# Sums of weight blocks by accumulating transfers in a seven-product FFN on one Trainium2 core

## The chip, the cores and the metric

The kernel runs on one core of a Trainium2 chip. The core has a matrix engine (TensorE, PE in the profile; its weight loads are PEld), VectorE (DVE), ScalarE (ACT), GpSimd (POOL) and SyncE (SP), which here only issues transfers. Sixteen DMA engines carry out the transfers of all queues. The metric is device microseconds of one execution; lower is better.

## The reference

One decoder layer over 256 tokens of width 2048: a SwiGLU FFN with half residual, a token mixer, a second such FFN, and a final norm. All is float32.

```python
D_MODEL = 2048; SEQ = 256; D_FF = 5632
def swiglu_ffn(x, w_gate, w_up, w_down):
    return (jax.nn.silu(x @ w_gate) * (x @ w_up)) @ w_down

x = x + 0.5 * swiglu_ffn(rms_norm(x, ffn1_norm), ffn1_w_gate, ffn1_w_up, ffn1_w_down)
z = rms_norm(x, mix_norm) @ w_in          # 2048 -> 5120, then RG-LRU and short conv
...
x = x + y @ w_out
x = x + 0.5 * swiglu_ffn(rms_norm(x, ffn2_norm), ffn2_w_gate, ffn2_w_up, ffn2_w_down)
return rms_norm(x, final_norm)
```

The change touches the two FFNs alone, and in them the products with the three weight matrices.

## The kernel before

**Precision by splitting.** A float32 matrix is split into a high part (ScalarE casts it to fp32r, the tiles `hi_`) and the rest (VectorE subtracts, the tiles `lo_`). A product is then made of three matmuls: both parts of the activations with the high part of the weights, and the high part of the activations with the low part of the weights. Weights are loaded in tiles of 512 rows by 512 columns (128 partitions x 4 x 512, 1 MB; a "unit" is 512 rows) by `load`, which issues one transfer on SP's queue; `parts_of` casts in two halves on ScalarE and makes the low part in one VectorE instruction of 2048 columns. Three sets of split tiles take turns (`splits_of`). Raw tiles come from a pool of three (`raws`) and, for the two that are kept and changed in place, a pool of two (`kept`, called w11 and w12).

**Blocks of seven products.** The FFNs take two token tiles (128 tokens each) by two units by two column tiles of 512 columns as a 2 x 2 by 2 x 2 block product, and make it with seven products of one token tile by one unit by one column tile where eight are usual. This needs sums of activations (made once, by `seven_of`) and sums of weights (made for each block, by `seven`). The weights of a block are w11, w12 (first unit, columns 0 and 1) and w21, w22 (second unit). Beside the seven products the block takes the remaining one or two units in the usual way (`usual`, both token tiles at once, the tiles `_x`), into the same four PSUM banks a, c, e, d. The order on PE is: product 0, product 4, usual 0 (columns 1), product 5, usual 1 (columns 1), product 6, product 2, usual 0 (columns 0), product 3, usual 1 (columns 0), product 1. The two `usual` calls of the second unit are left out where a block has one other unit. A product is 12 matmuls of 512 columns, 8 with the high and 4 with the low part; a usual unit is 24.

**The sums of weights before.** Product 4 takes w12 − w11, in place in w11 and in two halves of 1024 columns; product 5 takes w22 − that, again in w11; product 6 takes w22 − w12, in place in w12; product 3 takes w21 − w11, in place in w11. All five instructions are VectorE's. In the profile they are the TENSOR_TENSOR groups that write `raw_g`, `raw_u`, `raw_d` or `raw_g_first` from two raw tiles. The results of products 5 and 6 are copied from bank a to SBUF by ScalarE (`snap`: u2 and u3) and added later by `done`.

**How many.** For each FFN, ten blocks are gate and up products (columns 512 to 5632 in pairs, two other units each) and three are of the down projection (`down`, called after the first, third and fifth pair of columns; the first has one other unit, the later ones two). The first 512 columns of gate and up and part of the down projection are made without sums. That is 26 blocks in the kernel, 2 of them with one other unit.

**Order and waits.** A planner turns the program into one instruction list for each engine; each engine then runs its list in order and waits on semaphores. Nearly all instructions go through one helper, so their line in the profile is L43; SP's loads are L165 (`load`) and L208 (`part`, the transposes). GpSimd issues ten small transfers at the start (L109) and four memsets in the mixer. `order=True`, in two gate blocks of each FFN, pins a few VectorE instructions to program order; `ready` hands the first block of FFN 1 its w11 already split.

Of the kernel before, what the change touches and what calls it, by code (L numbers as in the profile page):

```python
# [13 lines left out]
AF = mybir.ActivationFunctionType  # L14
ALU = mybir.AluOpType
AX = mybir.AxisListType

P = 128
# [6 lines left out]
CW = 512  # L25
NC_D = D // CW
UK = 4
# [22 lines left out]
def hybrid_block(ctx: ExitStack, tc: tile.TileContext, a: dict, out: bass.AP):  # L50
    nc = tc.nc
    Engine.pinned = False
    dve, act, pe = (Engine(tc, e) for e in (nc.vector, nc.scalar, nc.tensor))
# [29 lines left out]
    def bank(name):  # L83
        return psum.tile([P, 512], F32, tag="ps", name=name)

    def f32(ap):
        return ap.bitcast(F32)
# [71 lines left out]
    def load(src, name, pieces=((0, UK),), loaded=None, kept=False):  # L159
        if kept:  # L160
            raw = extra[1].tile([P, UK, CW], F32, tag="kept", name=f"raw_{name}", bufs=2)
        else:
            raw = raws.tile([P, UK, CW], F32, tag="raw", name=f"raw_{name}")
        for i, e in pieces:
            nc.sync.dma_start(raw[:, i:e, :], src[i * P : e * P].rearrange("(j p) c -> p j c", p=P))  # L165
            if loaded:
                loaded(i)
        return raw

    def splits_of(name):  # L170
        pool, bufs = splits, 2
        if extra:
            turn_of["split"] += 1
            if turn_of["split"] % 3 == 0:
                pool, bufs = extra[0], 1
        hi = pool.tile([P, UK, CW], F32R, tag="hi", name=f"hi_{name}", bufs=bufs)
        lo = pool.tile([P, UK, CW], F32R, tag="lo", name=f"lo_{name}", bufs=bufs)
        return hi, lo, [(hi[:, j, :], lo[:, j, :]) for j in range(UK)]

    def parts_of(raw, name, pieces=((0, 2), (2, UK)), split=None):  # L180
        hi, lo, blk = splits_of(name)
        for i, e in pieces:
            if split:
                split(i)
            act.copy(hi[:, i:e, :], raw[:, i:e, :])
            if split:
                dve.tensor_tensor(lo[:, i:e, :], raw[:, i:e, :], f32(hi[:, i:e, :]), op=ALU.subtract)
        if not split:
            dve.tensor_tensor(lo, raw, f32(hi), op=ALU.subtract)
        return blk  # L190
# [4 lines left out]
    def stationary(tile, t):  # L195

        return [(tile[:, j, t * P : (t + 1) * P], tile[:, j, S + t * P : S + (t + 1) * P]) for j in range(UK)]
# [33 lines left out]
    def multiply(targets, blk, apart=False, middle=None):  # L231


        more = dict(skip_group_check=True) if apart else {}
        for ps, st, begin, _ in targets:
            for j in range(UK):
                pe.matmul(ps, st[j][0], blk[j][0], start=begin and j == 0, stop=False, **more)
                pe.matmul(ps, st[j][1], blk[j][0], start=False, stop=False, **more)
        if middle:
            middle()  # L240
        for ps, st, _, end in targets:
            for j in range(UK):
                pe.matmul(ps, st[j][0], blk[j][1], start=False, stop=end and j == UK - 1, **more)
        if len(targets) == NT:
            onward()
# [114 lines left out]
    def seven_of(sf, x0, x1, v, spare, parts, steps=None):  # L360

        a11, a12, a21, a22 = v[0, 0], v[0, 1], v[1, 0], v[1, 1]
        parts = iter(parts)

        def split(i, q):
            hi, lo = next(parts)
            act.copy(hi, q)
            dve.tensor_tensor(lo, q, f32(hi), op=ALU.subtract)  # L370
            sf[i] = [(hi[:, j, :], lo[:, j, :]) for j in range(UK)]

        sf.update({0: stationary(x0, 0), 1: stationary(x1, 0), 3: stationary(x1, 1)})
        dve.tensor_tensor(spare, a21, a22, op=ALU.add)
        split(4, spare)

        def adds():
            dve.tensor_tensor(a21, a11, a21, op=ALU.subtract)
            dve.tensor_tensor(a11, spare, a11, op=ALU.subtract)

        def rest():
            if steps is None:
                adds()
            split(5, a11)
            split(6, a21)
            dve.tensor_tensor(a12, a12, a11, op=ALU.subtract)
            split(2, a12)

        if steps is not None:
            steps.extend((adds, rest))  # L390
        return rest
# [1 line left out]
    def quad(tile):  # L393
        return tile.rearrange("p (j c) -> p j c", j=UK)

    def seven(w, rows, cols, sf, xs, name, keep, done, between=None, ready=None, whole=True, order=False):


        a, c, e, d = (bank(f"ps_{name}_{n}") for n in "aced")

        def get(u, n, kept=False):
            src = w[u * UK * P : (u + 1) * UK * P, cols[n] : cols[n] + CW]
            return load(src, f"{name}_{u}{n}", kept=kept)

        (r0, r1), two = rows, len(xs) > 1
        w11, first = ready or (get(r0, 0, True), None)
        w12 = get(r0, 1, True)
        b2, w22 = get(xs[0][0], 1), get(r1, 1)
        b3 = get(xs[1][0], 1) if two else None
        a2, w21 = get(xs[0][0], 0), get(r1, 0)  # L410
        a3 = get(xs[1][0], 0) if two else None

        def snap(ps, n):
            s = keep(f"{n}_{name}")
            act.copy(s, ps)
            return s

        def product_of(i, raw, ps, begin=False, end=True, blk=None):
            multiply([(ps, sf[i], begin, end)], blk or parts_of(raw, f"{name}_p{i}"), True)

        def usual(i, raw, n, *targets):

            blk = parts_of(raw, f"{name}_x{i}{n}")
            multiply([(ps, stationary(xs[i][1], t), b, z) for ps, t, b, z in targets], blk, True)

        product_of(0, w11, a, True, blk=first)
        s1 = None if whole else snap(a, "s1")
        if whole:
            act.copy(d, a)
        hi, lo, blk = splits_of(f"{name}_p4")  # L430
        for i in (0, 2):
            o = slice(i, i + 2)
            dve.tensor_tensor(w11[:, o], w12[:, o], w11[:, o], op=ALU.subtract)
            act.copy(hi[:, o], w11[:, o])
        for i in (0, 2):
            o = slice(i, i + 2)
            ins = dve.tensor_tensor(lo[:, o], w11[:, o], f32(hi[:, o]), op=ALU.subtract)
            if order:
                tc.keep_in_program_order(ins)
        product_of(4, w11, c, True, blk=blk)  # L440
        s5 = snap(c, "s5")
        if between:
            between(0)
        usual(0, b2, 1, (e, 1, True, not two), (c, 0, False, False))
        if between:
            between(1)
        dve.tensor_tensor(w11, w22, w11, op=ALU.subtract)
        product_of(5, w11, a)
        u2 = snap(a, "u2")
        if between:  # L450
            between(2)
        if two:
            usual(1, b3, 1, (e, 1, False, True), (c, 0, False, False))
        ins = dve.tensor_tensor(w12, w22, w12, op=ALU.subtract)
        if order:
            tc.keep_in_program_order(ins)
        product_of(6, w12, a)
        u3 = snap(a, "u3")
        done(1, 1, e, [u3, s5])
        product_of(2, w22, c)  # L460
        done(0, 1, c, [u2])
        usual(0, a2, 0, (d, 0, not whole, False), (a, 1, False, False))
        dve.tensor_tensor(w11, w21, w11, op=ALU.subtract)
        product_of(3, w11, a, end=not two)
        if two:
            usual(1, a3, 0, (a, 1, False, True), (d, 0, False, False))
        done(1, 0, a, [])
        product_of(1, w21, d)
        done(0, 0, d, [] if whole else [s1])

    def ffn(tag, norm, after, opening=False):
        with (
# [252 lines left out]
            def down(last):  # L725
# [64 lines left out]
                if tag == 1 and m == 5:  # L790
                    prepare()
                seven(
                    wd, (m, n), (2 * CW, CW), sh, [(u, hidden[u]) for u in others], f"d{tag}_{m}", keep, add,
                    within,
# [79 lines left out]
    with tc.tile_pool(name="mixer", bufs=1) as mp, tc.tile_pool(name="mixw", bufs=2) as mw:  # L874
# [208 lines left out]
        def row_factor(u):  # L1083
# [4 lines left out]
        order = [  # L1088
            (lru_x, 0, 0), (lru_x, 0, 1), (sc_c, 3, 0), (lru_gate, 1, 0), (sc_x, 4, 0),
            (lru_gate, 1, 1), (sc_c, 3, 1), (sc_x, 4, 1), (sc_b, 2, 0), (sc_b, 2, 1),  # L1090
        ]
        for i, (use, piece, half) in enumerate(order):
            between = row_factor if i == 0 else None
            ps = inward(w_in, piece * (D // 2) + half * CW, nm.xT, f"in_{piece}_{half}", between)
# [10 lines left out]
        for c, g in [(0, 0), (1, 0), (0, 1), (1, 1), (2, 0), (2, 1), (3, 0), (3, 1)]:  # L1105
# [3 lines left out]
            ps = product(w_out, c, (2 * g, 2 * g + 1), yT.__getitem__, f"o{c}_{g}", turn if (c, g) == (0, 1) else None)  # L1109
# [104 lines left out]
```

## Time and profile before

| | |
|---|---|
| median of 3 runs | 1709.46 us (1708.25 to 1712.31) |
| profiled execution | 1709.04 us |
| its span | 1707.3 us |
| PE busy | 1690.1 us (99%), 7471 matmuls |
| DVE busy | 1456.5 us (85%) |
| ACT busy | 1206.9 us (71%) |
| POOL busy | 6.3 us |
| DMA, SP's queue | 360.75 MB, 66.3% of 16 engines |
| HBM read | 339.82 MB |

Busy time is the time in which an engine had an instruction running. An engine that is off the path that sets the end may be busy without costing anything; what counts is who waits for whom. In a timeline row the first number is the start and the second the length in us, over as many instructions as "x" says; the bracket gives the idle time of the engine before it and what ended it.

### The profile page before, as it was taken

The page shows a single profiled execution, that of the slowest core. Times are in us where ns is not written, and L with a number is a line of the kernel's source. Part 1 is how long each engine was busy: PE and PEld are TensorE (multiplying, and loading weights), DVE is VectorE, ACT ScalarE, POOL GpSimd, SP SyncE. Part 2 cuts the span into 40 slices and gives each one's busy share as a digit, 9 for nine tenths or more (in the row PEclk, how much of TensorE's full clock was granted, in tenths as well). Part 3 has the DMA queues.
Part 4 walks back from the last instruction along what each step waited for, and adds up shares of the span by engine and source line. Part 5 has one row for each costly group of instructions (what it writes and reads, how often), then busy time and mean ns, then how long its engine had stood idle before and what let it go on. Part 6 is the DMA issues. An engine that isn't in the chain of part 4 may idle for free. (4 is left out here: it accounts for less than half of the span.)

```text
span 1707.3 us, 19494 instructions
## 1 busy us (share of the span) xinstructions
PE 1690.1 (99%) x7471; PEld 1394.7 (82%) x7471; DVE 1456.5 (85%) x1217; ACT 1206.9 (71%) x1501; POOL 6.3 (0%) x20
## 2 busy tenths in 40 slices
PE   8999999999999999999999999999999999999998
PEld 7888888888888888888888888888888888888886
DVE  7998988889889889668696679989989888889796
ACT  7867667776567678877877777685567765677764
POOL 1000000000000000000000000000000000000000
PEclk9999999999999999999999999999999999999999
DMA  8666567585567684875657694585666656576853
GB/s 307 205 230 197 197 222 222 182 276 189 191 202 206 233 270 131 258 216 191 213 190 221 191 301 161 198 271 185 222 213 205 220 188 222 197 216 203 248 196 123
DMA packets 254173, 363.11 MB, mean 213 GB/s; under 512 B 85892, under 2 KB 88320, under 8 KB 253952
## 3 DMA queue, kind: packets, MB, share of 16 engines
q1 hardware_dynamic: 253616, 360.75, 66.3%
q8 instruction: 58, 0.95, 0.2%
q10 hardware_dynamic: 144, 1.05, 0.2%
q14 instruction: 35, 0.29, 0.0%
q0 software_dynamic: 320, 0.07, 0.0%
HBM read 339.82 MB, written 2.10 MB: 200 GB/s over the span
## 5 line engine op out<-in xcount | busy, mean ns | idle before, releaser
L43 ACT CAST hi_u_p<-raw_u 128x1024 fp32r<-128x1024 f32 x140 | 141.5, 1047 | 56.8 <-DVE raw_u L43 27.1
L43 ACT CAST hi_g_p<-raw_g 128x1024 fp32r<-128x1024 f32 x132 | 134.0, 1047 | 57.8 <-DVE raw_g L43 26.1
L43 DVE TENSOR_TENSOR lo_u_p<-raw_u,hi_u_p 128x2048 fp32r<-128x2048 f32 (+1 forms) x80 | 160.0, 2019 | 14.7 <-ACT hi_u_p L43 14.2
L43 DVE TENSOR_TENSOR lo_g_p<-raw_g,hi_g_p 128x2048 fp32r<-128x2048 f32 (+1 forms) x75 | 151.7, 2031 | 20.4 <-ACT hi_g_p L43 19.7
L43 PE MATMUL ps_d<-hi_d,h 128*128 128x512 f32 x704 | 167.0, 389 | 0.0
L43 PEld LDWEIGHTS ps_d<-hi_d,h 128*128 128x128 f32 x704 | 132.1, 188 | 27.4
L43 PE MATMUL ps_in<-hi_in,xT_nm 128*128 128x512 f32 x640 | 151.9, 390 | 0.0
L43 PEld LDWEIGHTS ps_in<-hi_in,xT_nm 128*128 128x128 f32 x640 | 119.5, 188 | 24.6
L43 DVE TENSOR_TENSOR lo_in<-raw_in,hi_in 128x2048 fp32r<-128x2048 f32 x40 | 91.3, 2286 | 47.6 <-ACT hi_in L43 47.2
L43 ACT CAST hi_d_p<-raw_d 128x1024 fp32r<-128x1024 f32 x84 | 86.4, 1048 | 64.0 <-DVE raw_d L43 22.6
L43 DVE TENSOR_TENSOR lo_d<-raw_d,hi_d 128x2048 fp32r<-128x2048 f32 x44 | 100.2, 2288 | 34.0 <-ACT hi_d L43 33.9
L43 ACT CAST hi_u_x<-raw_u 128x1024 fp32r<-128x1024 f32 x80 | 81.2, 1047 | 38.6 <-PE ps_u_c L43 24.6
L43 DVE TENSOR_TENSOR lo_d_p<-raw_d,hi_d_p 128x2048 fp32r<-128x2048 f32 (+1 forms) x48 | 96.5, 2020 | 9.3 <-ACT hi_d_p L43 8.8
L43 ACT CAST hi_d<-raw_d 128x1024 fp32r<-128x1024 f32 x88 | 88.9, 1046 | 19.6 <-PE ps_d_d L43 7.6
L43 ACT CAST hi_in<-raw_in 128x1024 fp32r<-128x1024 f32 x80 | 80.8, 1046 | 30.3 <-PE ps_in L43 24.8
L43 DVE TENSOR_TENSOR raw_u<-raw_u,raw_u 128x2048 f32<-128x2048 f32 (+1 forms) x50 | 92.3, 1862 | 11.6 <-DMA raw_u<-in_ffn_w_up_dram 10.9
L43 DVE TENSOR_TENSOR lo_g_x<-raw_g,hi_g_x 128x2048 fp32r<-128x2048 f32 x40 | 91.4, 2285 | 9.2 <-ACT hi_g_x L43 9.1
L43 ACT CAST hi_g_x<-raw_g 128x1024 fp32r<-128x1024 f32 x80 | 81.2, 1046 | 22.3 <-PE ps_g_c L43 9.2
L43 DVE TENSOR_TENSOR lo_u_x<-raw_u,hi_u_x 128x2048 fp32r<-128x2048 f32 x40 | 91.4, 2284 | 1.3 <-ACT hi_u_x L43 1.1
L43 DVE TENSOR_TENSOR raw_g<-raw_g,raw_g 128x2048 f32<-128x2048 f32 (+1 forms) x46 | 84.9, 1868 | 4.7 <-DMA raw_g<-in_ffn_w_gate_dram 4.5
L43 PE MATMUL ps_d<-lo_d,h 128*128 128x512 f32 x352 | 87.3, 389 | 0.0
L43 PE MATMUL ps_in<-lo_in,xT_nm 128*128 128x512 f32 x320 | 79.0, 389 | 0.0
(402 smaller groups left out, 3661.4 us busy)
## 6 DMA issues: line engine op xcount, KB each, us to landing
raw_d<-in_ffn_w_down_dram SPq DMA_DIRECT2D x88, 1024.0 KB, 5.8
raw_u<-in_ffn_w_up_dram SPq DMA_DIRECT2D x87, 1024.0 KB, 5.3
raw_g<-in_ffn_w_gate_dram SPq DMA_DIRECT2D x86, 1024.0 KB, 5.3
raw_in<-in_w_in_dram SPq DMA_DIRECT2D x40, 1024.0 KB, 5.1
raw_o<-in_w_out_dram SPq DMA_DIRECT2D x16, 1024.0 KB, 5.9
xres<-in_x_dram SPq DMA_DIRECT2D x4, 512.0 KB, 7.6
raw_u<-in_ffn_w_up_dram SPq DMA_DIRECT2D x2, 512.0 KB, 9.3
raw_g_first<-in_ffn_w_gate_dram SPq DMA_DIRECT2D x1, 1024.0 KB, 12.0
```

Of the source, the lines that this page charges most:

```text
L43: ins = getattr(self.engine, name)(*args, **kwargs)
```

## The change

Signs are turned so that every sum of weights is an addition: the activations' sums take the other sign (`seven_of`: two instructions with another operator), and the results of products 5 and 6 are copied with a factor −1 (`snap` with `sign`, a scaled Copy on ScalarE in place of a copy). The sums of products 4 and 5 stay on VectorE. Those of product 6 (w12 += w22) and product 3 (w11 += w21) become accumulating transfers: `gather` issues, on GpSimd's queue, a transfer of the second weight tile from HBM that is added to the tile in SBUF. w22 and w21 are still loaded by SP as before, for products 2 and 1 and for the sum of product 5. The gather into w12 stands in the program ahead of product 4, that into w11 behind the snapshot of product 5. `fourth` has the default True, and no call passes another value. The pin of product 6's sum goes with its instruction.

```diff
@@ -371,7 +371,7 @@
             sf[i] = [(hi[:, j, :], lo[:, j, :]) for j in range(UK)]

         sf.update({0: stationary(x0, 0), 1: stationary(x1, 0), 3: stationary(x1, 1)})
-        dve.tensor_tensor(spare, a21, a22, op=ALU.add)
+        dve.tensor_tensor(spare, a21, a22, op=ALU.subtract)
         split(4, spare)

         def adds():
@@ -383,7 +383,7 @@
                 adds()
             split(5, a11)
             split(6, a21)
-            dve.tensor_tensor(a12, a12, a11, op=ALU.subtract)
+            dve.tensor_tensor(a12, a12, a11, op=ALU.add)
             split(2, a12)

         if steps is not None:
@@ -393,14 +393,19 @@
     def quad(tile):
         return tile.rearrange("p (j c) -> p j c", j=UK)

-    def seven(w, rows, cols, sf, xs, name, keep, done, between=None, ready=None, whole=True, order=False):
+    def seven(w, rows, cols, sf, xs, name, keep, done, between=None, ready=None, whole=True, order=False, fourth=True):


         a, c, e, d = (bank(f"ps_{name}_{n}") for n in "aced")

+        def of(u, n):
+            return w[u * UK * P : (u + 1) * UK * P, cols[n] : cols[n] + CW]
+
         def get(u, n, kept=False):
-            src = w[u * UK * P : (u + 1) * UK * P, cols[n] : cols[n] + CW]
-            return load(src, f"{name}_{u}{n}", kept=kept)
+            return load(of(u, n), f"{name}_{u}{n}", kept=kept)
+
+        def gather(to, u, n):
+            nc.gpsimd.dma_start(to, of(u, n).rearrange("(j p) c -> p j c", p=P), accum_op=ALU.add)

         (r0, r1), two = rows, len(xs) > 1
         w11, first = ready or (get(r0, 0, True), None)
@@ -410,9 +415,9 @@
         a2, w21 = get(xs[0][0], 0), get(r1, 0)
         a3 = get(xs[1][0], 0) if two else None

-        def snap(ps, n):
+        def snap(ps, n, sign=1.0):
             s = keep(f"{n}_{name}")
-            act.copy(s, ps)
+            act.activation(s, ps, AF.Copy, scale=sign)
             return s

         def product_of(i, raw, ps, begin=False, end=True, blk=None):
@@ -430,13 +435,14 @@
         hi, lo, blk = splits_of(f"{name}_p4")
         for i in (0, 2):
             o = slice(i, i + 2)
-            dve.tensor_tensor(w11[:, o], w12[:, o], w11[:, o], op=ALU.subtract)
+            dve.tensor_tensor(w11[:, o], w11[:, o], w12[:, o], op=ALU.add)
             act.copy(hi[:, o], w11[:, o])
         for i in (0, 2):
             o = slice(i, i + 2)
             ins = dve.tensor_tensor(lo[:, o], w11[:, o], f32(hi[:, o]), op=ALU.subtract)
             if order:
                 tc.keep_in_program_order(ins)
+        gather(w12, r1, 1)
         product_of(4, w11, c, True, blk=blk)
         s5 = snap(c, "s5")
         if between:
@@ -444,23 +450,23 @@
         usual(0, b2, 1, (e, 1, True, not two), (c, 0, False, False))
         if between:
             between(1)
-        dve.tensor_tensor(w11, w22, w11, op=ALU.subtract)
+        dve.tensor_tensor(w11, w11, w22, op=ALU.add)
         product_of(5, w11, a)
-        u2 = snap(a, "u2")
+        u2 = snap(a, "u2", -1.0)
+        if fourth:
+            gather(w11, r1, 0)
         if between:
             between(2)
         if two:
             usual(1, b3, 1, (e, 1, False, True), (c, 0, False, False))
-        ins = dve.tensor_tensor(w12, w22, w12, op=ALU.subtract)
-        if order:
-            tc.keep_in_program_order(ins)
         product_of(6, w12, a)
-        u3 = snap(a, "u3")
+        u3 = snap(a, "u3", -1.0)
         done(1, 1, e, [u3, s5])
         product_of(2, w22, c)
         done(0, 1, c, [u2])
         usual(0, a2, 0, (d, 0, not whole, False), (a, 1, False, False))
-        dve.tensor_tensor(w11, w21, w11, op=ALU.subtract)
+        if not fourth:
+            dve.tensor_tensor(w11, w11, w21, op=ALU.add)
         product_of(3, w11, a, end=not two)
         if two:
             usual(1, a3, 0, (a, 1, False, True), (d, 0, False, False))
```

## Prediction

> **What bounds the kernel now.** I read the page first (busy time, clock, DMA queues), then the waits of PE, then the windows of single blocks, then the timeline inside them. The page:
>
> ```profile
> span 1707.3 us, 19494 instructions
> ...
> PE 1690.1 (99%) x7471; PEld 1394.7 (82%) x7471; DVE 1456.5 (85%) x1217; ACT 1206.9 (71%) x1501; POOL 6.3 (0%) x20
> ...
> PEclk9999999999999999999999999999999999999999
> ```
>
> PE is busy for 1690.1 of 1707.3 us at full granted clock. The diff leaves every matmul in place, so a gain can only come out of the remaining 17.2 us. The waits of PE (who it waited for: us in total, times, longest) and the last matmul of the timeline split them:
>
> ```profile
> PE pt_n L43 <- DMA xres<-in_x_dram: 3.1, 1, 3.1
> PE pv_first L43 <- DMA rows_first<-in_ffn_norm_dram: 2.6, 1, 2.6
> PE ps_g_a L43 <- DVE lo_g_p L43: 1.5, 4, 0.4
> PE ps_u_c L43 <- DVE lo_u_p L43: 0.6, 1, 0.6
> PE ps_o L43 <- ACT hi_o L43: 0.3, 1, 0.3
> PE ps_o L43 <- DVE lo_o L43: 0.3, 1, 0.3
> PE ps_d_c L43 <- ACT s_d L43: 0.2, 1, 0.2
> 1697.70 1.07 PE L43 MATMUL ps_d<-lo_d,h 128*128 128x512 f32 x4
> ```
>
> The first two, 5.7 us, are the start; from 1698.8 to 1707.3 run 8.5 us of final norm and stores; neither is touched. 2.9 us are left in the middle, and only 2.1 of them (the two waits for DVE's lo_g_p and lo_u_p) lie in the blocks that change. DVE's 85% is thus a share of work hidden beside PE. Two blocks with four other loads and one with two (window, busy time and instructions of PE, PEld, DVE, ACT, POOL, then clock, DMA share, GB/s), and the DMA queue over the second:
>
> ```profile
> 200.46:241.26 40.80, 40.80 (x181) 33.78 (x180) 37.27 (x22) 25.53 (x30) 0.00 (x0) 1.00 0.61 206
> 241.26:282.06 40.80, 40.80 (x181) 33.78 (x180) 35.80 (x24) 27.42 (x31) 0.00 (x0) 1.00 0.68 219
> 1166.30:1196.20 29.90, 29.90 (x133) 24.60 (x132) 29.23 (x22) 19.85 (x24) 0.00 (x0) 1.00 0.64 210
> q1 hardware_dynamic: 6336, 8.91, 67.4%
> ```
>
> PE is busy for the whole of each, while DVE has some 10% and the DMA engines a third to spare.
>
> **The change, part by part.** There are 26 blocks: 24 of the long kind, and two short ones (the first `down` of each FFN, which has one other unit). *DVE.* A block now makes five sums, two of 1024 columns and three of 2048; the last two of the three leave DVE:
>
> ```profile
> L43 DVE TENSOR_TENSOR raw_u<-raw_u,raw_u 128x2048 f32<-128x2048 f32 x30 | 68.7, 2289 | 8.6 <-DMA raw_u<-in_ffn_w_up_dram 8.3
> L43 DVE TENSOR_TENSOR raw_g<-raw_g,raw_g 128x2048 f32<-128x2048 f32 x28 | 63.7, 2286 | 4.7 <-DMA raw_g<-in_ffn_w_gate_dram 4.5 <-DVE raw_g L43 0.2
> L43 DVE TENSOR_TENSOR raw_d<-raw_d,raw_d 128x2048 f32<-128x2048 f32 x18 | 41.2, 2290 | 1.8 <-DMA raw_d<-in_ffn_w_down_dram 1.4
> L43 DVE TENSOR_TENSOR raw_g_first<-raw_g,raw_g_first 128x2048 f32<-128x2048 f32 x2 | 4.6, 2282 | 0.0
> L43 DVE TENSOR_TENSOR raw_u<-raw_u,raw_u 128x1024 f32<-128x1024 f32 x20 | 23.6, 1222 | 3.0 <-DMA raw_u<-in_ffn_w_up_dram 2.7
> ```
>
> 30+28+18+2 = 78 = 26 x 3 wide sums, of which 52 go: 52 x 2.288 = 119 us, DVE from 1456 to about 1337 us. What that is worth on the path is bounded by 2.1 us. I take all of it: −2.1. *Signs.* Sum and difference in `seven_of` and the three sums that stay are the same instruction with another operator: 0. *Snapshots.* u2 and u3 become a scaled Copy:
>
> ```profile
> L43 ACT COPY u_u<-ps_u_a 128x512 f32<-128x512 f32 x20 | 11.6, 578 | 0.0
> L43 ACT ACTIVATE z<-ps_g_a 128x512 f32<-128x512 f32 x10 | 6.0, 600 | 31.3 <-PE ps_g_a L43 31.3
> L43 ACT CAST hi_u_p<-raw_u 128x1024 fp32r<-128x1024 f32 x140 | 141.5, 1047 | 56.8 <-DVE raw_u L43 27.1 <-issue 15.4 <-PE ps_u_a L43 12.0
> ```
>
> 52 x (600 − 578) ns = 1.1 us, hidden by ACT's idle third (25.53 of 40.80 us): 0; without that cover 1.1 us.
>
> *The gathers.* 52 accumulating transfers of 1 MB are added on POOL's queue; the plain loads of the same tiles stay on SP's, and none is moved. POOL has nothing else to do within the FFNs (its busy time is 6.3 us). Each gather is a new wait: for product 6 it starts when the two half sums have read w12, for product 3 when the low part of product 5 has been made, and the ACT casts of that product wait for its landing. Behind them in ACT's order stand the casts of the next units, behind those DVE's low parts, behind those PE; and the slot of w11 or w12, so SP's next kept load, comes free later by as much. How late may it land? After it come two casts (2 x 1.047 us) and a low part of 2.29 us, 4.4 us together, and PE needs the low part 1.8 us after the product's first matmul. From the timeline, the tightest regular block and the short one:
>
> ```profile
> 279.89 2.35 DVE L43 TENSOR_TENSOR raw_g<-raw_g,raw_g 128x1024 f32<-128x1024 f32 x2
> 292.92 2.29 DVE L43 TENSOR_TENSOR lo_g_p<-raw_g,hi_g_p 128x2048 fp32r<-128x2048 f32 x1 [0.31 <-ACT hi_g_p L43]
> 301.74 1.98 PE L43 MATMUL ps_g_a<-hi_g_p,xs 128*128 128x512 f32 x8
> 303.56 1.07 PE L43 MATMUL ps_g_a<-lo_g_p,xs 128*128 128x512 f32 x4
> 312.62 1.98 PE L43 MATMUL ps_g_a<-hi_g_p,x 128*128 128x512 f32 x8
> ...
> 1174.13 2.29 DVE L43 TENSOR_TENSOR lo_d_p<-raw_d,hi_d_p 128x2048 fp32r<-128x2048 f32 x1 [0.25 <-ACT hi_d_p L43]
> 1190.89 1.98 PE L43 MATMUL ps_d_a<-hi_d_p,h 128*128 128x512 f32 x8
> ```
>
> Product 6 starts at 301.74, its tile is free at 282.24: room 301.74 + 1.8 − 4.4 − 282.24 = 16.9 us. Product 3: 312.62 + 1.8 − 4.4 − 295.21 = 14.8 us. In the short block product 3 has 1190.89 + 1.8 − 4.4 − 1176.42 = 11.9 us. So 14.8 us (and twice 11.9) is the price limit of a gather. No row of this kernel shows an accumulating transfer. The nearest are plain loads and POOL's small ones (KB each, median us to landing):
>
> ```profile
> raw_g<-in_ffn_w_gate_dram SPq DMA_DIRECT2D x86, 1024.0 KB, 5.3
> raw_g_first<-in_ffn_w_gate_dram SPq DMA_DIRECT2D x1, 1024.0 KB, 12.0
> rows_first<-in_ffn_norm_dram SPq DMA_DIRECT2D x1, 8.0 KB, 1.7
> rows_many<-in_lru_conv_b_dram POOLq DMA_DIRECT2D x1, 4.0 KB, 6.0
> rows_conv<-in_lru_conv_w_dram POOLq DMA_DIRECT2D x1, 16.0 KB, 5.3
> ```
>
> Low end: 5.3 us, as a plain load: all hidden, even in the short blocks. High end: POOL's slowest small transfer and the slowest 1 MB load, 6.0 + 12.0 = 18.0 us: 24 x (18.0 − 14.8) + 2 x (18.0 − 11.9) = 89 us. Between them I take 5.3 us for POOL's path, and for 1 MB what a load takes beyond a small one on SP, 5.3 − 1.7 = 3.6 us, twice, as the old sum must be read as well as the weights: 5.3 + 7.2 = 12.5 us. It is nearer to the rows than the crowded 12.0 us, which is of the start, where everything is loaded at once. That is within 14.8; the short blocks lose 2 x (12.5 − 11.9) = 1.2 us.
>
> The collectives page of the Trainium skill (Collectives: The Full Stack, The bandwidth ceiling) gives the same reason for the doubling: an add inside a transfer is slow for its two source reads, not for the adding. By its measured ratio of 1.93 the landing would be 5.3 + 6.9 = 12.2 us, an estimate, and the short blocks would lose 0.6 us. No run here shows it yet.
>
> *The DMA engines.* 8.91 MB take 67.4% of a block, so 1.05 MB take 7.9%. Two gathers add 16% as plain traffic, to 83%, and 32% if doubled, to 99%. This counts waiting inside packets as work, so it is a ceiling; the loads' bursts can be moved by some us, as three sets of split tiles let ACT run ahead of PE. I take 0 and keep the full engines as a rival.
>
> **The sum.** −2.1 + 0 + 0 + 1.2 + 0 = −0.9 on the profiled execution's 1709.04 us (span 1707.3 and 1.7 us around it); the median of the runs is 1709.46, 0.4 more. So 1708.1 to 1708.6; I say 1708.6: no change that a measurement of this kernel could tell (0.2%, 3.4 us).
>
> **The rivals.** *Late gather (the other side).* Place: the cast of product 3, behind it PE. It decides from a landing of 14.8 us on, and every us beyond costs 24 us and more: at 16 us 24 x 1.2 + 2 x 4.1 = 37 us, 1746; at 18.0 us 1798. For it: the landing has no row, and POOL must write the descriptors of 512 rows of 2 KB where its small transfers had 8 to 32 rows. Against it: 2.3 us remain at my value. *Full DMA engines.* At 99% loads land late and each casts late; if 3% of a block were lost, 24 x 40.8 x 0.03 = 29 us, 1738; at a threefold price, 115%, 15% of it, 147 us, 1856. For it: the waits of DVE and ACT for landing weights that exist already (8.3 us of raw_u above). Against: a third of the engines' time is idle now. *The gain.* DVE relieved by 10% lets the split run further ahead, and all 2.9 us go without a new wait: 1709.0 − 2.9 = 1706.1; with luck in the start or end below the 0.2%. *DVE holds up POOL.* A POOL issue takes half a microsecond:
>
> ```profile
> 6.32 0.52 POOL L109 DMA_DIRECT2D rows_conv<-in_lru_conv_w_dram  x1 [0.55 <-DMA rows_many<-in_mix_norm_dram]
> ```
>
> If it advanced only while DVE is idle (some 12% of a block), it would take 0.52 / 0.12 = 4.3 us, the landing would be 12.5 + 3.8 = 16.3 us, and 24 x 1.5 + 2 x 4.4 = 45 us are lost: 1754. Against it: (2289 − 1222) ns for 1024 more columns is 1.04 ns a column, DVE's plain pace in these sums and low parts. SBUF — State Buffer in the Trainium skill (Who interferes with whom) has this lock: descriptors from GpSimd starve while DVE runs in a two-port mode, but tensor_tensor has no such mode; by that the rival falls, and no run here shows it.
>
> That the sums do not leave DVE at all can't be: the diff has no call with `fourth` off.
>
> **How the numbers follow.** Hidden 0.48; late gather 0.22; full engines 0.20; DVE's hold 0.05; gain 0.05. The last is faster, the three before it slower: faster 0.05, same 0.48, slower 0.47. The likeliest, hidden, gives 1708.6, its own range 1706.1 to 1712. The range goes up to 1765, which takes in all of DVE's hold and four fifths of the late gather and two thirds of the full engines (out: 0.04 and 0.07), and down to 1705.5 (out: 0.03).
>
> **What would show it.** Right: PE's waits in the blocks still a few us, DVE near 1337 us, 52 POOL transfers landing in 9 to 14 us, the DMA share of a long block 0.80 to 0.95. Wrong: PE waiting for hi_ or lo_ parts of products 3 and 6 with ACT waiting on a POOL transfer (late gather); waits spread over all products with ACT waiting on SP's loads (full engines); POOL issues of several us beside busy DVE (the hold).

## The result and the profile after

The changed kernel takes 1720.14 us (median of 5 runs, 1718.53 to 1725.6) against 1709.46: ratio 1.007 (1.0057 to 1.0084), 0.7% slower where no change was forecast. The page of its profiled execution (1720.14 us), the lines that answer to those of before:

```profile
span 1718.4 us, 19630 instructions
...
PE 1691.8 (98%) x7471; PEld 1394.0 (81%) x7471; DVE 1353.3 (79%) x1165; ACT 1204.9 (70%) x1501; POOL 73.8 (4%) x72
...
q1 hardware_dynamic: 253616, 360.75, 64.5%
q0 software_dynamic: 27776, 54.60, 19.0%
```

PE has the same work at a granted clock of 0.998 where it was 0.999 and stands idle 26.6 us instead of 17.2; its busy time is 1.7 us longer. VectorE lost 52 instructions and 103 us. What is new is queue q0, GpSimd's: 54.6 MB take 19.0% of the 16 engines' span. The waits of PE in the changed kernel (us in total, times, longest):

```profile
PE ps_u_c L43 <- ACT s_u L43: 6.3, 7, 2.4
PE pt_n L43 <- DMA xres<-in_x_dram: 3.5, 1, 3.5
PE pv_first L43 <- POOL ident masks.py:199: 2.5, 1, 2.5
PE ps_g_a L43 <- DVE lo_g_p L43: 2.0, 4, 0.7
PE ps_in L43 <- ACT hi_in L43: 1.5, 1, 1.5
PE ps_g_c L43 <- ACT s_g L43: 0.8, 1, 0.8
```

The start (pt_n, pv_first) is about as before, 6.0 us for 5.7; the middle grew from 2.9 to 12.0 us (1.4 of it in five smaller rows), and its largest entry is new: PE wants to write bank c again (`ps_u_c`) and ScalarE has not yet copied it out (`s_u`, the snapshot s5 of product 4). No row is a wait for the parts of product 3 or 6 (the waits for lo_g_p are product 5's, as before). Two neighbouring long blocks, gate and up, and the queues over the second (windows; columns as before):

```profile
204.06:244.86 40.80, 40.80 (x182) 33.79 (x180) 31.25 (x20) 24.13 (x29) 1.56 (x2) 1.00 0.87 257
244.86:287.03 42.17, 41.09 (x181) 33.71 (x180) 33.08 (x22) 27.96 (x32) 2.59 (x2) 1.00 0.94 262
q1 hardware_dynamic: 6339, 8.92, 64.0%
q0 software_dynamic: 1056, 2.10, 29.7%
```

The first block still takes 40.80 us, the second loses 1.37 us at a DMA share of 0.94. The transfers (issue to landing) and ScalarE's waits for them:

```profile
raw_d<-in_ffn_w_down_dram SPq DMA_DIRECT2D x88, 1024.0 KB, 6.3
raw_u<-in_ffn_w_up_dram SPq DMA_DIRECT2D x87, 1024.0 KB, 7.0
raw_g<-in_ffn_w_gate_dram SPq DMA_DIRECT2D x86, 1024.0 KB, 7.2
raw_u<-in_ffn_w_up_dram POOLq DMA_DIRECT2D x20, 1024.0 KB, 9.1
raw_g<-in_ffn_w_gate_dram POOLq DMA_DIRECT2D x19, 1024.0 KB, 9.3
ACT hi_g_x L43 <- DMA raw_g<-in_ffn_w_gate_dram: 20.7, 10, 4.1
ACT hi_u_x L43 <- DMA raw_u<-in_ffn_w_up_dram: 15.5, 7, 3.1
ACT hi_g_p L43 <- DMA raw_g<-in_ffn_w_gate_dram: 12.9, 6, 2.6
ACT hi_d_p L43 <- DMA raw_d<-in_ffn_w_down_dram: 3.9, 2, 2.5
```

The `_x` rows are SP's plain loads, of which those of raw_u and raw_g land 1.7 to 1.9 us later than before (5.3 us). The `_p` rows, with one more of 2.9 us for `raw_g_first`, are gathers: 19.7 us in nine waits, seven for product 3 in gate blocks, one for product 6 in the first short down block (1.4 us) and one for product 3 in the second (2.6 us).

### The profile page after: what moved, and what is told of

Its sections match the earlier page's. It is cut to its first block, busy times and chain, and to the rows that moved or that the text cites. A ratio compares the mean times of both kernels' runs of the same rounds, so it can differ in the third digit from the quotient of the medians.

```text
span 1718.4 us, 19630 instructions
## 1 busy us (share of the span) xinstructions
PE 1691.8 (98%) x7471; PEld 1394.0 (81%) x7471; DVE 1353.3 (79%) x1165; ACT 1204.9 (70%) x1501; POOL 73.8 (4%) x72
## 3 DMA queue, kind: packets, MB, share of 16 engines
q0 software_dynamic: 27776, 54.60, 19.0%
## 5 line engine op out<-in xcount | busy, mean ns | idle before, releaser
L43 PEld LDWEIGHTS ps_d<-lo_d,h 128*128 128x128 f32 x352 | 66.1, 188 | 13.7
L43 PEld LDWEIGHTS ps_in<-lo_in,xT_nm 128*128 128x128 f32 x320 | 60.1, 188 | 12.5
```

What stands on the lines that cost most here:

```text
L43: ins = getattr(self.engine, name)(*args, **kwargs)
```

## One stretch, followed from the gather to PE

The first gate block and the up block behind it show how the two reach PE. The rows of the changed kernel: POOL's issue of product 3's gather, rows of ScalarE and VectorE (timeline), the landing of the SP load issued at 76.86 us, and PE in the up block:

```profile
70.10 1.30 POOL L408 DMA_DIRECT2D raw_g_first<-in_ffn_w_gate_dram  x1 [10.42 <-DVE lo_g_p L43]
81.16 1.05 ACT L43 CAST hi_g_p<-raw_g_first 128x1024 fp32r<-128x1024 f32 x1 [2.86 <-DMA raw_g_first<-in_ffn_w_gate_dram]
87.14 2.00 ACT L43 CAST hi_g_x<-raw_g 128x1024 fp32r<-128x1024 f32 x2 [2.31 <-DMA raw_g<-in_ffn_w_gate_dram]
89.17 2.29 DVE L43 TENSOR_TENSOR lo_g_x<-raw_g,hi_g_x 128x2048 fp32r<-128x2048 f32 x1 [2.21 <-ACT hi_g_x L43]
93.97 0.60 ACT L43 ACTIVATE z<-ps_g_a 128x512 f32<-128x512 f32 x1 [0.52 <-PE ps_g_a L43]
103.75 1.99 ACT L43 CAST hi_u_p<-raw_u 128x1024 fp32r<-128x1024 f32 x2 [1.13 <-DVE raw_u L43]
106.60 0.59 ACT L43 ACTIVATE s_u<-ps_u_c 128x512 f32<-128x512 f32 x1
raw_g<-in_ffn_w_gate_dram SPq DMA_DIRECT2D x1, 1024.0 KB, 10.2
107.24 2.11 PE L43 MATMUL ps_u_c<-hi_u_x,x 128*128 128x512 f32 x8 [2.43 <-ACT s_u L43]
```

The gather lands 11.0 us after its issue and ScalarE stands 2.86 us; then a plain load, issued 6.8 us behind the gather, lands after 10.2 us and it stands another 2.31 us. ScalarE itself has made this up by `z` at 93.97, where it waits for PE. VectorE has not: from its low part of the late load at 89.17 to its sum for product 5 at 101.39 it is never idle for more than 0.13 us, so it hands the delay on. The casts of product 5 wait for that sum, the copy `s_u` stands behind them in ScalarE's list, and PE loses 2.43 us at bank c. All seven of PE's waits for `s_u` come behind such a wait for a plain load in the gate block ahead (1.6 to 4.1 us). The same rows of the kernel of e7, whose lists of instructions are in the same order and which waits for small transfers in place of the gather, 9.6 us from first issue to cast against 11.1:

```profile
69.99 1.29 POOL L410 DMA_DIRECT2D raw_g_first<-in_ffn_w_gate_dram  x1 [6.70 <-DVE lo_g_p L43]
79.64 1.05 ACT L43 CAST hi_g_p<-raw_g_first 128x1024 fp32r<-128x1024 f32 x1 [1.83 <-DMA raw_g_first<-in_ffn_w_gate_dram]
83.21 1.98 ACT L43 CAST hi_g_x<-raw_g 128x1024 fp32r<-128x1024 f32 x2
85.35 2.28 DVE L43 TENSOR_TENSOR lo_g_x<-raw_g,hi_g_x 128x2048 fp32r<-128x2048 f32 x1
93.58 0.60 ACT L43 ACTIVATE z<-ps_g_a 128x512 f32<-128x512 f32 x1 [3.39 <-PE ps_g_a L43]
100.41 2.00 ACT L43 CAST hi_u_p<-raw_u 128x1024 fp32r<-128x1024 f32 x2
103.25 0.60 ACT L43 ACTIVATE s_u<-ps_u_c 128x512 f32<-128x512 f32 x1
raw_g<-in_ffn_w_gate_dram SPq DMA_DIRECT2D x1, 1024.0 KB, 6.1
104.26 1.98 PE L43 MATMUL ps_u_c<-hi_u_x,x 128*128 128x512 f32 x8
```

Here the plain load lands after 6.1 us, ScalarE does not wait for it, and PE does not wait for `s_u`. Of the 3.8 us by which VectorE's low part is later in the changed kernel, 1.5 are there at the cast of product 3 already (81.16 against 79.64); the rest comes from the plain load.

## The experiments

Each ratio is to the kernel before, run beside it on the same chip (its medians there: 1708.94 for e1 to e4, 1708.66 for e5 to e8, 1709.15 for e9 to e12, 1708.63 us for e13 to e15).

**e1: the snapshot of bank c ahead of product 5's casts.**

```diff
-        s5 = snap(c, "s5")
+        s5 = keep(f"s5_{name}")
+        taken = act.activation(s5, c, AF.Copy, scale=1.0)
...
-        product_of(5, w11, a)
+        with tc.issue_after(taken.ins):
+            product_of(5, w11, a)
```

> The changed kernel with ScalarE's two casts of product 5 held behind the snapshot s5 of product 4 in ScalarE's order; nothing else is edited. Order theory: the 8.7 us that PE waits at the first use of bank c after product 4 come from the order alone, because the planner now puts these casts ahead of s5 in all ten up blocks; with s5 first they go, and the time falls to 1710 to 1713 us. Supply theory: the 54.6 MB of added traffic make every load late (5.3 to 7.0 us for raw_u), and s5 only happens to be where the lateness shows; the wait moves to the casts and low parts of product 5, and the time stays at 1717 to 1721 us.

1731.49 us, 1.0135 (1.012 to 1.0151). The order theory falls: with the snapshot early it is slower still. Product 5's casts come later, so w11 is free later, and in the up blocks product 3's gather is issued 8.2 us behind the first matmul of product 4 where it was 6.4 (medians, from the trace); ScalarE's waits for gathers grow from 19.7 to 58 us and those for SP's loads of the usual units (the `_x` rows) from 38 to 90 us. `s_u` looks like the place where the lateness came out, not its source; e1 alone does not show that, since it moves the gather too, but e7 does, with the list unchanged.

**e2: signs and scaled copies alone** (no gathers; both sums additions on VectorE).

```diff
-        gather(w12, r1, 1)
...
+        dve.tensor_tensor(w12, w12, w22, op=ALU.add)
         product_of(6, w12, a)
```

(and `fourth=False`, which puts the sum of product 3 back on VectorE.)

> The changed kernel with both gathers taken out and both sums made by VectorE again, as additions; the turned signs and the scaled copies stay. Both theories: 1708 to 1711 us, as before, since neither the order on ScalarE nor the traffic differs from the kernel before. If the scaled copies cost something on the path, 1711 us or more.

1709.22 us, 1.0004 (0.9995 to 1.0013): turned signs and scaled copies cost nothing that shows (at most 0.13%).

**e3: neither gathers nor sums for products 6 and 3.**

> The changed kernel without the gathers and without any sum for products 6 and 3, which take the tiles as they stand (the output is another one): VectorE is relieved as in the changed kernel, the traffic is that of before, and the planner again puts the casts of product 5 ahead of s5 in all ten up blocks. Order theory: PE still waits for s5, 6 to 9 us in all, 1715 to 1719 us. Supply theory: no late loads, no wait, 1706 to 1709 us. If it takes both, an order that is harmless as long as ScalarE is on time: 1707 to 1711 us.

1706.73 us, 0.9988 (0.9979 to 0.9997). This is what VectorE's relief is worth, 2.2 us, and about all that a version which moves these sums elsewhere has to gain.

**e4: only product 6's gather; e5: only product 3's** (the other sum on VectorE).

> The changed kernel with the gather of product 6 alone; the sum of product 3 is VectorE's. The order on ScalarE has the casts ahead of s5 in all ten up blocks, the added traffic is half. Order theory: 1716 to 1720 us, as the changed kernel. Supply theory: half of the loss, 1713 to 1716 us. Both needed: 1711 to 1716 us.

> The gather of product 3 alone; product 6's sum is an addition on VectorE again. Half the traffic, as in the kernel with product 6's gather alone (1710.3 us), but it is the gather whose landing ScalarE waited for: in the changed kernel the nine casts that waited for a gather (19.7 us of ScalarE's time in all) are nearly all of product 3. Wait theory (the loss is the landing of product 3's gather, late in ScalarE's order): most of the 11 us stays, 1716 to 1719 us. Traffic theory (the loss is the DMA engines' load by both gathers, and grows faster than the load): as product 6's gather alone, 1709 to 1711 us, with SP's loads of raw_g and raw_u landing in 5.3 to 5.8 us.

e4: 1710.33 us, 1.0009 (1.0 to 1.0017), although ScalarE waits 43 us for SP's plain loads there, more than the 38 of the changed kernel: the sum of such waits is no measure of the loss. e5: 1733.53 us, 1.014 (1.0125 to 1.0155), far beyond what either theory gave, and more than both gathers together. The two load the engines alike (q0 9.5% and 9.4%). In e5 ScalarE's list is another one, and it waits 57 us for gathers, in the up blocks too (`hi_u_p` 37.7 us, 10 times), where the changed kernel does not wait at all; there the gather is issued 10.0 us behind the first matmul of product 4 and not 6.4. So neither traffic nor the changed kernel's 19.7 us of waits is the whole account: the order that the planner makes decides when a gather starts and how much of its landing ScalarE sees.

**e6: gathers that overwrite instead of adding.**

```diff
-..., accum_op=ALU.add)
+...)
```

> Both gathers without the accumulation: each transfer overwrites its tile, so that the sums for products 6 and 3 are left out and the output is not the reference's. Every engine's instructions are those of the changed kernel, in the same order, with the same waits. If the DMA engines charge an accumulating transfer about double (19.0% of the span for 54.6 MB, against 64.5% for 360.75 MB), the gather queue's share falls to about 9.7%, and a transfer lands about 1 to 2 us earlier, in 7 to 8 us. Traffic theory: most of the loss goes, 1708 to 1712 us. Wait theory: a landing that is 1 to 2 us shorter takes away 9 to 18 us of the nine waits' 19.7 us, so that it too gives 1709 to 1713 us; what this run settles is the share of the loss that the accumulation itself causes. If it stays above 1716 us, neither the doubling nor the landing matters, but the count of transfers.

1712.48 us (1707.04 to 1716.62), 1.0016 (1.0006 to 1.0026). Same lists, same 1 MB transfers:

```profile
q0 software_dynamic: 14464, 54.60, 9.7%
raw_u<-in_ffn_w_up_dram POOLq DMA_DIRECT2D x20, 1024.0 KB, 5.6
```

Adding takes twice the packets and twice the engines' time (19.0% against 9.7%) and 3.5 us of landing. Without it no cast waits for a gather, SP's loads still land in 5.7 to 6.4 us and ScalarE still waits 27 us for them; 3.8 of the 10.7 us of loss are left, though its own runs lie 10 us apart.

**e7: the wait without the traffic**, two small accumulating transfers in a row for each gather.

```diff
+            src = of(u, n).rearrange("(j p) c -> p j c", p=P)
+            for _ in range(2):
+                nc.gpsimd.dma_start(to[:, :, :16], src[:, :, :16], accum_op=ALU.add)
```

> Wait without traffic: in place of each gather two small accumulating transfers one behind the other into 16 of the 512 columns of each row group (32 KB each, the second waits for the first, since they write the same place), so that the sums for products 6 and 3 are left out for the other columns and the output is not the reference's. The products' casts still wait for the landing of the second; from the small GpSimd transfers (5 to 6 us from issue to landing) two in a row should take 9 to 12 us, about what a whole gather took (9.1 us). Wait theory: the loss stays, 1716 to 1722 us. Traffic theory: SP's loads land in 5.3 us again and the time is that of the kernel with no gathers and no sums, 1706.5 to 1708.5 us.

1709.15 us, 1.0003 (0.9994 to 1.0011). ScalarE waits for gathers as in the changed kernel (19.6 against 19.7 us), and from first issue to last landing those of product 3 in the gate blocks take 10.5 us (median, from the issues and landings in the trace) against 10.3. In the up blocks and for product 6 the small pair is quicker than a gather (medians 7.5 against 10.2 us, and 6.4 to 6.9 against 8.6 to 8.7), but there ScalarE waits for gathers only once in the changed kernel, 1.4 us. SP's loads of raw_u and raw_g land in 5.3 and 5.4 us, ScalarE's waits for those of the usual units are gone, and so are 11.0 us. This is the cleanest comparison of the study: same lists, about the same waits for the gathers, without the bytes.

**e8: product 3 one unit later.**

```diff
-        product_of(3, w11, a, end=not two)
         if two:
-            usual(1, a3, 0, (a, 1, False, True), (d, 0, False, False))
+            usual(1, a3, 0, (a, 1, False, False), (d, 0, False, False))
+        product_of(3, w11, a)
```

> Traffic without product 3's wait: both gathers whole, but product 3 stands one unit (about 10 us of TensorE) later, behind the second other unit of the column, so that its cast has 10 us more before it needs the gather. Wait theory: 1708 to 1711 us. Traffic theory: 1716 to 1720 us. Side effect to be seen in the trace: w11's kept slot comes free some 10 us later, so that the next block's first load may be late; if the time is above 1722 us it is that, with ScalarE or VectorE waiting for SP's load ahead of product 0, and the run tells nothing on the two theories.

1771.35 us, 1.0363 (1.0349 to 1.0376). It is above 1722 us, the case set apart: by the edit w11's slot comes free one unit later, and VectorE, which does not wait for SP's loads in the changed kernel, does so here (`raw_u` 15.1 us; 10.9 in the kernel before). It tells nothing on the two theories.

**e9: three small transfers in a row.** The edit is e7's with `range(3)`.

> Wait without traffic, now as long as a whole gather: three small accumulating transfers in a row (32 KB each, one waits for the other) in place of each gather; the sums for products 6 and 3 are left out for the other columns, so that the output is not the reference's. Order of every engine as in the changed kernel. With two in a row (3.1 us median each) ScalarE waited 19.6 us for them, as long as for the whole gathers (19.7 us), and the time was 1709.15 us. Three take some 9.5 us, or up to 13 us where the first is delayed. Traffic theory: 1709 to 1712 us. Wait theory: 1716 us and more.

1836.61 us, 1.0745 (1.0727 to 1.0762): against the traffic theory, and the largest loss of all, while SP's loads of raw_u and raw_g land in 5.3 and 5.4 us. The first gate block (POOL's first issue, ScalarE's cast), and then the waits of PE:

```profile
73.10 1.29 POOL L410 DMA_DIRECT2D raw_g_first<-in_ffn_w_gate_dram  x1 [2.71 <-issue]
89.69 1.04 ACT L43 CAST hi_g_p<-raw_g_first 128x1024 fp32r<-128x1024 f32 x1 [8.30 <-DMA raw_g_first<-in_ffn_w_gate_dram]
PE ps_g_a L43 <- ACT u_g L43: 38.8, 9, 7.0
PE ps_u_a L43 <- ACT u_u L43: 31.6, 10, 5.0
```

With 16.6 us from first issue to cast (medians to the last landing 15.7 and 16.8 us in gate and up blocks) instead of 10 or 11 the wait becomes the bound. And PE does not wait for product 3's parts: it waits for `u_g` and `u_u`, the snapshot u3 of bank a, which stands behind the waiting cast in ScalarE's list. Not all of the loss is waiting: of the 126 us between the profiled executions of e7 and e9, 36 are PE's own busy time (1689.6 to 1725.4 us), at a granted clock of 0.979 against 0.998.

**e10: half gathers** (256 of 512 columns: `to[:, :, : CW // 2]`).

> Half the accumulating traffic, in the same order: both gathers, each for 256 of the 512 columns of a row group (512 KB), the other columns' sums left out, so that the output is not the reference's. Traffic theory: between the two small transfers (1709.15 us) and the whole gathers (1720.1 us), 1712 to 1716 us, with ScalarE's waits for SP's loads of raw_g and raw_u between 0 and 36 us. Wait theory: as the waits for the gathers go; a landing of about 7 us leaves the time at 1707 to 1710 us.

1708.54 us, 1.0 (0.9991 to 1.0008): 5.6 to 6.6 us for SP's loads, 6.0 us for a gather, no waits for gathers. Halving the transfers takes away the whole loss, not half of it; the traffic theory's 1712 to 1716 was too high.

**e11 and e12: the orders of e5 and e1 with two small transfers for each gather.**

> The kernel with product 3's gather alone (1733.5 us), its order of all engines kept, but two small transfers in a row (32 KB each) in place of the gather: no traffic, still a wait; product 3's sum is left out for the other columns, so that the output is not the reference's. If that kernel's order alone costs what it lost: 1725 us and more. If the order is only vulnerable, and the loads that collide with the gathers (SP's landing 6.2 to 6.5 us against 5.3) turn it into stalls: 1708 to 1712 us.

> The changed kernel with the snapshot of bank c put ahead of product 5's casts (1731.5 us), order kept, and two small transfers in a row (32 KB each) in place of each gather; the sums for products 6 and 3 are left out for the other columns, so that the output is not the reference's. The order alone at fault: 1722 us and more. Order only vulnerable to late loads and late gathers: 1707 to 1712 us.

e11: 1720.7 us, 1.0069 (1.0056 to 1.0083). e12: 1721.77 us, 1.0075 (1.0062 to 1.0089). Neither expectation was met: 12.8 and 9.7 us go with the traffic, and some 12 us stay. What stays comes with waits for the small transfers, 40 us of ScalarE's time in e11 and 73 in e12, at 9.5 to 11.5 us from first issue to last landing (medians of product 3's). No run has these lists without any gather, so it is not shown how much of the 12 us is the wait and how much the order by itself.

**e13: product 5's parts asked for earlier, gathers whole; e14: the same with two small transfers.**

```diff
+        dve.tensor_tensor(w11, w11, w22, op=ALU.add)
+        five = parts_of(w11, f"{name}_p5")
         usual(0, b2, 1, (e, 1, True, not two), (c, 0, False, False))
...
-        dve.tensor_tensor(w11, w11, w22, op=ALU.add)
-        product_of(5, w11, a)
+        product_of(5, w11, a, blk=five)
```

> The changed kernel with the sum, casts and low part of product 5 asked for ahead of the first other unit instead of behind it, so that w11 is free and the gather for product 3 starts about 3 us earlier in the gate blocks. Both gathers whole. If ScalarE's waits for the gathers (19.7 us in the changed kernel) are needed for the loss, it goes with them: 1708 to 1712 us. If the late loads alone carry it (ScalarE's waits for SP's loads of the FFNs' weights 38 us in the changed kernel): 1716 to 1722 us, with the waits for the gathers near 0.

> The same early order of product 5, with two small transfers in a row (32 KB each) in place of each gather; the sums for products 6 and 3 are left out for the other columns, so that the output is not the reference's. This prices the order by itself, without traffic and with a gather time of about 6.5 us: 1706.5 to 1709 us if the order is as good as the changed kernel's (1709.15 us with the same small transfers), 1715 us and more if it is one of the vulnerable orders.

e13: 1741.99 us, 1.0195 (1.0181 to 1.0209). e14: 1719.06 us, 1.0062 (1.0049 to 1.0074). ScalarE's waits for transfers of FFN weights in e13 (the longest in total), then in e14:

```profile
ACT hi_u_x L43 <- DMA raw_u<-in_ffn_w_up_dram: 57.1, 19, 5.2
...
ACT hi_g_x L43 <- DMA raw_g<-in_ffn_w_gate_dram: 8.8, 5, 2.4
ACT hi_u_x L43 <- DMA raw_u<-in_ffn_w_up_dram: 2.8, 2, 1.7
ACT hi_g_p L43 <- DMA raw_g<-in_ffn_w_gate_dram: 2.2, 1, 2.2
```

The waits for the gathers are gone in both (one of 1.0 us and one of 2.2 us), as the edit meant. Yet the whole gathers cost 22.9 us more than the small ones: in this list late loads are enough for a loss. The order by itself is some 10 us worse than the changed kernel's (1719.06 against 1709.15 us with the same small transfers), which was not expected either.

**e15: half gathers, the other columns summed on VectorE** (the reference's sums).

```diff
+        dve.tensor_tensor(w12[:, :, CW // 2 :], w12[:, :, CW // 2 :], w22[:, :, CW // 2 :], op=ALU.add)
         product_of(6, w12, a)
...
+        o = slice(CW // 2 if fourth else 0, CW)
+        dve.tensor_tensor(w11[:, :, o], w11[:, :, o], w21[:, :, o], op=ALU.add)
```

> The reference's output, with gathers of half the size: each gathers 256 of the 512 columns of a row group, and VectorE adds the other half (26 x 2 sums of 1024 columns, 1.22 us each, 63 us of its time instead of 119). With half gathers alone the time was 1708.5 us. Both theories: 1707 to 1711 us, the same as before within 0.2%; if the planner's new order is a vulnerable one, 1713 us and more, with ScalarE's waits for gathers and loads above 50 us.

1716.8 us, 1.0043 (1.0031 to 1.0056): the planner makes yet another list, and VectorE waits 52 us for SP's loads. No version that computes the reference's result and moves a sum beat the kernel before, and by e3 there are 2.2 us to be had, 0.13%.

**What the runs say together.** The same list, with whole gathers and with two small transfers of about the same wait:

| list of | whole | small | whole − small |
|---|---|---|---|
| the changed kernel | 1720.14 | 1709.15 (e7) | 11.0 |
| e1 | 1731.49 | 1721.77 (e12) | 9.7 |
| e5 (one gather in a block) | 1733.53 | 1720.70 (e11) | 12.8 |
| e13 | 1741.99 | 1719.06 (e14) | 22.9 |

In all four the bytes cost 9.7 us or more. In the changed kernel they are the loss: with the waits kept and the bytes gone it stands at the time before. The wait by itself costs at most 2.4 us there (e7 against e3, which also holds what the small transfers load on the engines); at 16 us it cost over 100 (e9). Three things stay open. The lists of e1, e5 and e13 do worse than the changed kernel's even with the small transfers; in e1 and e5 the gather starts 1.7 and 3.6 us later in the up blocks, but in e13 it does not, and the loss is not traced to single instructions. No run has the changed kernel's list with all the bytes and no wait for the gathers, so it is not shown that the bytes alone would cost the 11 us there. And it is not told apart how much comes from the load on the engines as such and how much from its doubling: e6 leaves 3.8 us without the doubling, with a spread of 10 us between runs, while e10 takes more of the engines (10.9% against 9.7%) and loses nothing.

## Why the prediction was wrong

- **The step that failed: "The DMA engines ... I take 0".** It was argued that bursts can be moved by some us, since three sets of split tiles let ScalarE run ahead. The measured term is +11.0 us (e7). The loads had little lead to be moved in: in the kernel before, ScalarE already waited 18.7 us for plain loads of usual units in gate and up blocks (lines below); in the changed kernel it is 36.2, for 1.7 to 1.9 us more of landing on the median and 10.2 for 6.1 us in the stretch shown. And what room there was, was ScalarE's: it caught up, while VectorE, in a run without gaps, carried the delay on to the casts ahead of `s_u`. The set-aside rival, full engines, was right that ScalarE would wait for SP's loads, and its 99% is 94% in the up block shown; PE's waits did not spread over all products but stand mostly at bank c, and its price, 3% of a block, was too high: 1738 against 1720.

```profile
ACT hi_u_x L43 <- DMA raw_u<-in_ffn_w_up_dram: 11.2, 9, 1.9
ACT hi_g_x L43 <- DMA raw_g<-in_ffn_w_gate_dram: 7.5, 6, 1.9
```

- **What stands behind the wait.** The prediction followed cast, low part, PE, and found 14.8 us of room for a landing. It left out the snapshots in ScalarE's list, which give PSUM banks back to PE. They are where PE waits in the changed kernel (`s_u`) and in e9 (`u_g`, `u_u`). The runs do not contradict the limit itself, since it lies between 10.5 us (e7, harmless) and 16 us (e9), but they place it no closer; beyond it the price is 127 us from e7 to e9 where the late-gather rival gave 37 us at 16 us.
- **The landing**, estimated 12.5 us, is 8.9 to 9.3 us in the median, 11.0 at most. The doubling was right (19.0% for 9.7%), the 5.3 us for GpSimd's path were too much: a small transfer in e7 lands in 3.1 us. Of the range given, 9 to 14 us, it is the lower edge. The short blocks' 1.2 us: ScalarE waits 1.4 us for product 6's gather in the first and 2.6 us for product 3's in the second, and PE does not wait in either.
- **VectorE's relief, −2.1 us**: the size is right, −2.2 (e3), but by luck. The four waits for lo_g_p, 1.5 of the 2.1 us, were to go and still stand in e3 (1.4 us); only the 0.6 us for lo_u_p are gone there. VectorE's busy time fell by 103 us and not by 119: the 52 sums and their 119 us are gone from the groups, but busy time counts overlapping ends once, and back-to-back instructions overlap (68 us in all before, 54 after).
- **Signs and snapshots, 0**: right (e2); the scaled copies of u_u and u_g take 589 and 591 ns where the copies took 578 and 582.
- **DVE's hold on POOL, 0.05**: it did not come. An accumulating issue takes 1.30 us in every group while VectorE is busy 79% of the time.

```profile
L408 POOL DMA_DIRECT2D raw_u<-in_ffn_w_up_dram x20 | 25.9, 1297 | 357.8 <-ACT hi_u_p L43 275.8 <-DVE lo_u_p L43 82.0
L43 ACT ACTIVATE u_g<-ps_g_a 128x512 f32<-128x512 f32 x20 | 11.8, 591 | 0.0
```

That VectorE's tensor_tensor has no two-port mode and was not seen to stall transfers is also what the Trainium skill says (SBUF — State Buffer, Who interferes with whom), though it adds that with both inputs in SBUF it contends with GpSimd's reads. The trace agrees that no transfer's issue was held up. The Trainium skill has a ratio of 1.93 between two collectives, without and with an add inside the transfer (Collectives: The Full Stack, The bandwidth ceiling). The 1.96 here, 19.0% over 9.7%, agrees with it.

## What to carry to other kernels

A DMA share below one was no cover for added transfers here, where loads are issued as their buffers come free: ask what each load's landing becomes when it meets the new transfer, who stands still for the difference, and which engine next in the chain has no gap in which to make it up, whatever its mean busy share. When an instruction on an in-order engine is given a new wait, list everything behind it on that engine, the copies that give PSUM banks back above all, and not only the data that the wait is about. Here the sums of 2.3 us on an engine that PE hardly waits for were worth 2.2 us in all, and paying for them with memory traffic was a loss.

## What was not expected of the hardware

- An accumulating transfer of 1 MB with rows of 2 KB counts 528 packets (27776 less 320 of other work, over 52) where an overwriting one counts 272, takes 1.96 times the engines' time, lands in 9.1 instead of 5.6 us, and its issue on GpSimd takes 1.30 instead of 0.75 us.
- Its price does not go by bytes alone: e7's 104 transfers of 512 rows of 64 B take 6.1% of the engines' span for 3.49 MB; the half gathers of e10, rows of 1 KB, take 10.9% for 27.34 MB where the whole ones take 19.0% for 54.60 MB.
